# Two products for three where an expert has few tokens, a branch around the third, and experts in pairs

## The chip, the cores and the metric

The kernel runs on one core of one Trainium2 chip. The metric is the device time of one execution in microseconds: a median over runs. The engines of a core that matter here are TensorE (PE, matrix products), VectorE (DVE), ScalarE (ACT) and GpSimd (POOL); each takes its own instructions in the order in which the program put them, and they wait for each other by semaphores. SyncE (SP) issues the transfers of the weights. A profile of one execution shows each instruction's start, duration and what ended the wait ahead of it.

## The reference

A trunk of two pre-norm layers over 256 tokens of width 1024, in float32. Each layer has a token mixer and a channel mixer; the channel mixer of layer 0 is a dense SwiGLU, that of layer 1 chooses two of eight expert SwiGLUs for every token. Each expert has gate and up matrices of 1024 x 3584 and a down matrix of 3584 x 1024:

```
def swiglu(h, w_gate, w_up, w_down):
    return (jax.nn.silu(h @ w_gate) * (h @ w_up)) @ w_down

def moe_ffn(h, router_w, router_b, w_gate, w_up, w_down):
    logits = t.astype(jnp.float32) @ router_w.astype(jnp.float32) + router_b.astype(jnp.float32)
    top_v, top_i = lax.top_k(logits, TOP_K)
    gates = jax.nn.softmax(top_v, axis=-1)
    combine = jnp.sum(jax.nn.one_hot(top_i, N_EXPERTS, dtype=jnp.float32) * gates[..., None], axis=1)
    ...
        y_e = swiglu(t, w_gate[e], w_up[e], w_down[e])
        out = out + combine[:, e:e + 1] * y_e.astype(jnp.float32)
```

The router gives eight counts of tokens that add up to 512. The kernel computes an expert only for its own tokens, in 128 slots; a branch at the end takes care of counts over 128.

## The kernel before

**Products.** A product in float32 precision is made of three products in a rounded type (fp32r): both operands are split into a high and a low part, and `mm3` (lines 152 to 155) adds high x high (L153), low x high (L154) and high x low (L155) in one PSUM bank. In the expert stage the activations are the operand that is loaded (128 x 128), the weights the one that streams (512 columns).

**Weights.** All weights come in blocks of 1 MB into a ring of tiles (`raw`, 11 and 3 more), issued by SP (L104). A block is two pieces. `w_conv` turns a piece into a high part `wh`, a cast on ACT (L119), and a low part `wl` = raw − wh on DVE (L122), each in a ring of four (`NWC`). The first 24 pieces of the experts and the very last ones have a third of the low part done on POOL (L124). `piece` hands out the next piece and converts as far ahead as the rings go.

**Experts.** For each expert, the 3584 hidden columns are seven panels of 512. A panel has three steps of four pieces each: G (gate), D (down, of the panel before) and U (up), in that order (`panel_steps`); the eight experts come one after the other, 56 panels in all. G and U take 24 products each into one bank (`Ge`, `Ue`), D adds 24 into two banks (`edn`) that live through an expert's panels. In the middle of G, `trans` turns the hidden activations of the panel before with four PE transposes (`tre`, L248), and ACT and DVE split the result into `ehh` (L252) and `ehl` (L253). ACT applies silu to `Ge` with the slots' 1/rms as scale (`esg`, L768), and DVE multiplies that by the scaled `Ue` (`eh`, L783).

**Around it.** `one_hot` makes a 0/1 matrix of tokens and slots for a pair of experts, `gather` fetches the pair's tokens by products with it (L686, L687) and splits them into `xte`, `one_hot_T` transposes it; `scatter` takes an expert's results back to the tokens (L712, L713) and adds them, weighted, on DVE (L714). The gathers of the next pair are placed in the second expert's panels. At the end `overflow` loads the largest count (L842) and branches (L843).

The order on each engine is made when the program is built: code in the order in which it is written, except where a scheduler moves instructions of different engines against each other by priority.

## Time and profile before

| | |
|---|---|
| median of 3 runs | 1427.29 us (1425.96 to 1427.61) |
| profiled execution | 1422.7 us of span, 4.6 us around it |
| mean granted clock of PE | 0.993 |
| PE busy | 1391.0 us (98%) |
| DVE busy | 1188.3 us (84%) |
| ACT busy | 968.5 us (68%) |
| POOL busy | 113.6 us (8%) |
| moved by DMA | 428.26 MB, mean 301 GB/s |

Busy times are sums over the whole span. The expert stage is the stretch from 425 to 1409 us; the mixers and the dense layer come before it. Matmuls overlap, so that a busy PE says only that one was under way; the distance between the starts of two of them tells what one costs.

### The profile page before, as it was taken

The numbers are of one execution on the slowest core, as the hardware profiler recorded it, in microseconds if no ns is written. First come the engines' busy times: TensorE is split into PE (matmuls) and PEld (weight loads), VectorE is DVE, ScalarE is ACT, GpSimd is POOL, SyncE is SP. The second block draws the span as 40 slices with busy tenths as digits, with TensorE's granted clock in tenths as the row PEclk, the third lists the DMA queues.
The fourth block names the chain that finished last, engine by engine and source line by source line (L and its number), as shares of the span: only waits on it lengthen the run. The fifth ranks groups of instructions, "written<-read, shape, count | busy, mean of one in ns | idle before, by whom it ended". The sixth has DMA issues, their size and how long they took to land.

```text
span 1422.7 us, 19229 instructions
## 1 busy us (share of the span) xinstructions
PE 1391.0 (98%) x7115; PEld 1173.6 (82%) x7115; DVE 1188.3 (84%) x1304; ACT 968.5 (68%) x1136; POOL 113.6 (8%) x106
## 2 busy tenths in 40 slices
PE   7999999999979999999999999999999999999996
PEld 6989999998957888888888887888887888888884
DVE  6775555558878999999998988999998899999996
ACT  5554444445448887888787777777777777777775
POOL 2311000000338000000000000000000000000002
PEclk9999999999989999999999999999999999999998
DMA  9945555555447999999999999999998999899960
GB/s 364 368 174 178 182 196 184 178 190 186 161 175 265 356 369 373 345 355 351 357 371 356 351 344 350 348 353 370 375 357 335 349 356 350 344 419 359 364 250 32
DMA packets 61301, 428.26 MB, mean 301 GB/s; under 512 B 6928, under 2 KB 7440, under 8 KB 10000
## 3 DMA queue, kind: packets, MB, share of 16 engines
q1 hardware_dynamic: 59904, 424.86, 79.1%
q10 hardware_dynamic: 1008, 1.97, 0.4%
q8 instruction: 57, 0.93, 0.3%
q14 instruction: 44, 0.36, 0.1%
q0 software_dynamic: 288, 0.14, 0.0%
HBM read 425.89 MB, written 1.05 MB: 300 GB/s over the span
## 4 chain that ended last, share of the span: by engine, by line
PE 91%; DVE 4%; issue 2%; ACT 1%; DMA 1%; POOL 0%; ACTq 0%; POOLq 0%; DVEq 0%
PE Ue L155 7%; PE Ue L153 7%; PE Ue L154 7%; PE Ge L153 7%; PE Ge L155 7%; PE Ge L154 7%; PE edn L154 6%; PE edn L155 6%; PE edn L153 6%; DVE wl L122 2%; PE U L295 2%; PE U L294 2%; PE U L293 2%; PE dn L154 2%; PE dn L153 2%; PE dn L155 2%
## 5 line engine op out<-in xcount | busy, mean ns | idle before, releaser
L122 DVE TENSOR_TENSOR wl<-raw,wh 128x1024 fp32r<-128x1024 f32 (+1 forms) x802 | 954.7, 1227 | 147.3 <-ACT wh L119 135.6
L119 ACT CAST wh<-raw 128x1024 fp32r<-128x1024 f32 (+1 forms) x806 | 824.9, 1051 | 290.2 <-PE Ue L154 61.2
L153 PE MATMUL Ge<-wh,xte 128*128 128x512 f32 x448 | 180.5, 403 | 0.0
L155 PE MATMUL Ue<-wl,xte 128*128 128x512 f32 x448 | 175.9, 393 | 3.0 <-DVE wl L122 3.0
L154 PE MATMUL edn<-wh,ehl 128*128 128x512 f32 x448 | 175.0, 391 | 1.6 <-DVE ehl L253 1.6
L155 PE MATMUL Ge<-wl,xte 128*128 128x512 f32 x448 | 175.6, 392 | 0.0
L153 PE MATMUL edn<-wh,ehh 128*128 128x512 f32 x448 | 175.0, 391 | 0.0
L153 PE MATMUL Ue<-wh,xte 128*128 128x512 f32 x448 | 174.6, 390 | 0.0
L154 PE MATMUL Ue<-wh,xte 128*128 128x512 f32 x448 | 174.4, 389 | 0.0
L154 PE MATMUL Ge<-wh,xte 128*128 128x512 f32 x448 | 174.4, 389 | 0.0
L155 PE MATMUL edn<-wl,ehh 128*128 128x512 f32 x448 | 164.3, 393 | 0.2 <-DVE wl L122 0.2
L124 POOL TENSOR_TENSOR wl<-raw,wh 128x320 fp32r<-128x320 f32 x28 | 38.4, 1397 | 962.0 <-PE edn L154 941.2
L155 PEld LDWEIGHTS Ue<-wl,xte 128*128 128x128 f32 x448 | 84.1, 188 | 25.3 <-DVE wl L122 8.1
L155 PEld LDWEIGHTS edn<-wl,ehh 128*128 128x128 f32 x448 | 83.5, 188 | 21.8 <-DVE wl L122 3.6
L154 PEld LDWEIGHTS edn<-wh,ehl 128*128 128x128 f32 x448 | 84.1, 188 | 19.3 <-DVE ehl L253 2.4
L155 PEld LDWEIGHTS Ge<-wl,xte 128*128 128x128 f32 x448 | 84.1, 188 | 18.8
L154 PEld LDWEIGHTS Ue<-wh,xte 128*128 128x128 f32 x448 | 84.1, 188 | 17.5
L153 PEld LDWEIGHTS edn<-wh,ehh 128*128 128x128 f32 x448 | 84.2, 188 | 17.1 <-ACT wh L119 0.2
L153 PEld LDWEIGHTS Ue<-wh,xte 128*128 128x128 f32 x448 | 84.1, 188 | 16.9
L154 PEld LDWEIGHTS Ge<-wh,xte 128*128 128x128 f32 x448 | 84.4, 188 | 16.2
L153 PEld LDWEIGHTS Ge<-wh,xte 128*128 128x128 f32 x448 | 84.2, 188 | 15.6
L252 ACT CAST ehh<-tre 128x512 fp32r<-128x512 f32 x56 | 32.7, 585 | 83.9 <-PE tre L248 83.9
(328 smaller groups left out, 1936.9 us busy)
## 6 DMA issues: line engine op xcount, KB each, us to landing
raw<-in_m_gate_dram SPq DMA_DIRECT2D x112, 1024.0 KB, 7.0
raw<-in_m_up_dram SPq DMA_DIRECT2D x112, 1024.0 KB, 6.5
raw<-in_m_down_dram SPq DMA_DIRECT2D x111, 1024.0 KB, 7.1
raw<-in_w_in_dram SPq DMA_DIRECT2D x15, 1024.0 KB, 5.4
raw<-in_w_gate_dram SPq DMA_DIRECT2D x14, 1024.0 KB, 4.8
raw<-in_w_up_dram SPq DMA_DIRECT2D x14, 1024.0 KB, 4.9
raw<-in_w_down_dram SPq DMA_DIRECT2D x14, 1024.0 KB, 4.8
raw<-in_w_out_dram SPq DMA_DIRECT2D x8, 1024.0 KB, 10.9
```

Of the source, the lines that this page charges most:

```text
L119: nc.scalar.copy(h[:, q], r[:, q])
L122: e.tensor_tensor(lo[:, :cut], r[:, :cut], h[:, :cut].bitcast(F32), op=ALU.subtract)
L124: nc.gpsimd.tensor_tensor(lo[:, cut:], r[:, cut:], h[:, cut:].bitcast(F32), op=ALU.subtract)
L153: nc.tensor.matmul(o, xh, wh, start=start, stop=False)
L154: nc.tensor.matmul(o, xl, wh, start=False, stop=False)
L155: nc.tensor.matmul(o, xh, wl, start=False, stop=stop)
L252: return (nc.scalar.copy(hi, pt), nc.vector.tensor_tensor(lo, pt, hi.bitcast(F32), op=ALU.subtract))
L293: nc.tensor.matmul(o, wh[:, k], hT[:, k], start=k == 0, stop=False)
L294: nc.tensor.matmul(o, wh[:, k], lT[:, k], start=False, stop=False)
L295: nc.tensor.matmul(o, wl[:, k], hT[:, k], start=False, stop=k == KD - 1)
```

## The change

An expert with at most 64 tokens is called light, the others heavy. For a light expert the slots 64 to 127 repeat its tokens (`posm` gets a second form, `one_hot`). Its gathered operand then gets the high parts in slots 0 to 63 and the low parts in slots 64 to 127 (`fold`: ACT scales the second half by `heavy`, DVE adds the low part times `light`). A product of that operand with a piece of weights gives high and low results in different rows of one pass, so that passes with `wh` and `wl` do what three did. The third pass is put in a branch on the expert's count (`third`): eight products that a heavy expert takes and a light one skips. The count of each expert is loaded into PE's registers ahead of the first expert (L829).

The two halves of the rows have to be added. G's and U's results are copied from PSUM by ACT (`eG`, `eU`, L855) and turned with `turn`: eight products in full float32 with a matrix `E` that transposes, adds the halves and applies 1/rms. Silu (L784) and the multiplication (`eh`, L785) come after that. `ehh` and `ehl` are split as before, and a further instruction on DVE (L790) puts the low part into the second half of `ehh` for a light expert.

The steps now run G, U, D (of the panel before), and the two experts of a pair take turns, panel by panel. The rings change: 7 blocks of weights (and 3 more), 8 high parts, 5 low parts, 10 tiles of 512 columns. The results of the two experts are scattered together; the weight of a token is applied to the slots. POOL's share of the first 24 pieces is gone.

```diff
-    NRAW, NWC, NXT = 11, 4, 3
+    NRAW, NWC, NWH = 7, 5, 8
...
-        flat = [(e, n) for e in range(n_exp) for n in range(NPAN)]
+        if n_exp == 1:
+            flat = [(0, n) for n in range(NPAN)]
+        else:
+
+            flat = [(2 * p + j, n) for p in range(n_exp // 2) for n in range(NPAN) for j in range(2)]
         for i, (e, n) in enumerate(flat):
             last = i == len(flat) - 1
             steps.append(("G", e, n))
-            if not last and i > 0:
+            if n_exp == 1 and not last and i > 0:
                 steps.append(("D",) + flat[i - 1])
             steps.append(("U", e, n))
+            if i > 0 and (last or n_exp > 1):
+                steps.append(("D",) + flat[i - 1])
             if last:
-                steps.append(("D",) + flat[i - 1])
                 steps.append(("D", e, n))
         return steps
...
-            h = wp.tile([P, 1024], F32R, tag="wh", name=f"wh{i}", bufs=NWC)
+            h = wp.tile([P, 1024], F32R, tag="wh", name=f"wh{i}", bufs=NWH)
             lo = wp.tile([P, 1024], F32R, tag="wl", name=f"wl{i}", bufs=NWC)
...
-            cut = 704 if i >= 2 * NW - 4 else 704 if moe0 <= i < moe0 + 24 else 1024
+            cut = 704 if i >= 2 * NW - 4 else 1024
...
+        nc.vector.tensor_scalar(light, pr[:, 16:24], 64.5, None, op0=ALU.is_lt)
+        nc.vector.scalar_tensor_tensor(posm[:, :, :, 0], selb, -OFF, pr[:, :16].rearrange("p (b e) -> p b e", b=NB),
                                        op0=ALU.mult, op1=ALU.add)
+        nc.vector.scalar_tensor_tensor(posm[:, :, :, 1], light.unsqueeze(1).to_broadcast([P, NB, NE]), 64.0,
+                                       posm[:, :, :, 0], op0=ALU.mult, op1=ALU.add)
...
         S = sb.tile([P, NB, 2, P], F32R, tag="S", name=f"S{nm}{p}", bufs=1)
-        for b in range(NB):
-            for j in range(2):
-                e = 2 * p + j
-                nc.vector.tensor_scalar(S[:, b, j], iot, posm[:, b, e:e + 1], None, op0=ALU.is_equal)
+        io = iotam.rearrange("p (h t) -> p h t", h=2).unsqueeze(1).to_broadcast([P, 2, 2, 64])
+        for b in range(NB):
+            nc.vector.tensor_tensor(S[:, b].rearrange("p j (h t) -> p j h t", h=2), io,
+                                    posm[:, b, 2 * p:2 * p + 2].unsqueeze(3).to_broadcast([P, 2, 2, 64]),
+                                    op=ALU.is_equal)
...
+        et = sb.tile([P, P], F32, tag="et", name=f"et{nm}", bufs=1)
+        nc.vector.scalar_tensor_tensor(et, swap, light[:, e:e + 1], ident, op0=ALU.mult, op1=ALU.add)
+        E = sb.tile([P, P], F32, tag="E", name=f"E{nm}", bufs=4)
+        nc.vector.tensor_scalar(E, et, rs[:, :1], None, op0=ALU.mult)
+        return ST, rs, E
...
+    def fold(X, e):
+
+        q = (slice(None), slice(None), e % 2, slice(64, P))
+        nc.scalar.activation(X[0][q], X[0][q].bitcast(F32), AF.Copy, scale=heavy[:, e:e + 1])
+        nc.vector.scalar_tensor_tensor(X[0][q], X[1][q].bitcast(F32), light[:, e:e + 1], X[0][q].bitcast(F32),
+                                       op0=ALU.mult, op1=ALU.add)
...
+        def turn(e, n):
+
+            g, u = gs.pop((e, n)), us.pop((e, n))
+            pg, pu = bank("mm", f"gt{e}{n}"), bank("mm", f"ut{e}{n}")
+            for src, o in ((g, pg), (u, pu)):
+                for c in range(4):
+                    q = slice(c * P, (c + 1) * P)
+                    nc.tensor.matmul(o[:, q], src[:, q], E[e], start=True, stop=True)
+            sg, ht = t2(f"esg{e}{n}"), t2(f"eh{e}{n}")
+            nc.scalar.activation(sg, pg, AF.Silu)
+            nc.vector.tensor_tensor(ht, pu, sg, op=ALU.mult)
             hh = t2(f"ehh{e}{n}", F32R).rearrange("p (c t) -> p c t", c=4)
             hl = t2(f"ehl{e}{n}", F32R).rearrange("p (c t) -> p c t", c=4)
-            split(hh, hl, pt.rearrange("p (c t) -> p c t", c=4))
+            h = ht.rearrange("p (c t) -> p c t", c=4)
+            split(hh, hl, h)
+            nc.vector.scalar_tensor_tensor(hh[:, :, 64:], hh[:, :, 64:].bitcast(F32), nlight[:, e:e + 1], h[:, :, 64:],
+                                           op0=ALU.mult, op1=ALU.add)
             hTs[e, n] = (hh, hl)
...
+        def third(e, todo):
+
+            with tc.If(cnt[e] > 64):
+                for o, a, w in todo:
+                    nc.tensor.matmul(o, a, w, start=False, stop=False)
...
         with tc.high_priority():
             begin(0)
             for i in range(4):
                 chunks(0, i)
+            nc.vector.tensor_scalar(heavy, light, -1.0, 1.0, op0=ALU.mult, op1=ALU.add)
+            nc.vector.tensor_copy(cnti, pr[:, 16:24])
+            for e in range(2):
+                fold(X[0], e)
+        nc.vector.tensor_scalar(nlight, light, -1.0, None, op0=ALU.mult)
+        for e in range(NE):
+            cnt[e] = nc.values_load(cnti[0:1, e:e + 1], engines=[mybir.EngineType.PE], min_val=0, max_val=T)
...
             if kind in "GU":
                 pp = bank("mm", f"{kind}e{e}{n}")
+                todo = []
                 for kh in range(4):
                     wh, wl = piece(2)
                     for k in range(2):
-                        kk = kh * 2 + k
-                        mm3(pp, xt[e][:, 0, kk], xt[e][:, 1, kk], wh[:, k], wl[:, k], kk == 0, kk == KD - 1)
-                    if kh == 1 and prev is None:
+                        mm(pp, X[p][0][:, kh * 2 + k, j], wh[:, k], start=kh + k == 0, stop=False)
+                        todo.append((pp, X[p][1][:, kh * 2 + k, j], wh[:, k]))
+                    for k in range(1 if kh == 3 else 2):
+                        mm(pp, X[p][0][:, kh * 2 + k, j], wl[:, k], start=False, stop=False)
+                    if kh == 1:
+                        if kind == "G" and prev is not None:
+                            turn(*prev)
+                        if ready:
+                            (i, ys), more = ready[0], ready[1:]
+                            scatter(ys(), i, f"e{e}")
+                            ready = [(i2, early(y2)) for i2, y2 in more]
+                third(e, todo)
+                mm(pp, X[p][0][:, KD - 1, j], wl[:, 1], start=False, stop=True)
+                t = t2(f"e{kind}{e}{n}")
+                nc.scalar.copy(t, pp)
+                if kind == "G":
+                    gs[e, n] = t
...
+                else:
+                    us[e, n] = t
+                    if e == 0 and n == 0:
+                        route_rest(pr)
                         rest(0)
-                    if kh == 1 and kind == "G" and prev is not None:
-                        trans(*prev)
...
-                if kind == "G":
-                    gt = t2(f"esg{e}{n}")
-                    nc.scalar.activation(gt, pp, AF.Silu, scale=rs[e])
-                    gact[e, n] = gt
...
-                else:
-                    ht = t2(f"eh{e}{n}")
-                    nc.vector.scalar_tensor_tensor(ht, pp, rs[e], gact.pop((e, n)), op0=ALU.mult, op1=ALU.mult)
-                    hs[e, n] = ht
                     prev = (e, n)
...
+            todo = []
             for kk in range(4):
                 wh, wl = piece(1)
                 for i in range(2):
                     q = slice(i * 512, (i + 1) * 512)
-                    mm3(acc[e][i], hh[:, kk], hl[:, kk], wh[:, 0, q], wl[:, 0, q],
-                        n == 0 and kk == 0, n == NPAN - 1 and kk == 3)
-            if n == NPAN - 1:
+                    mm(acc[e][i], hh[:, kk], wh[:, 0, q], start=n == 0 and kk == 0, stop=False)
+                    todo.append((acc[e][i], hl[:, kk], wh[:, 0, q]))
+                if kk < 3:
+                    for i in range(2):
+                        mm(acc[e][i], hh[:, kk], wl[:, 0, i * 512:(i + 1) * 512], start=False, stop=False)
+                if kk == 1 and e == NE - 2 and n == NPAN - 1:
+                    turn(*prev)
+            third(e, todo)
+            for i in range(2):
+                mm(acc[e][i], hh[:, 3], wl[:, 0, i * 512:(i + 1) * 512], start=False, stop=n == NPAN - 1)
```

How instructions stand now is shown at three places. The first is ACT's queue. Before: the casts of G's four pieces (`wh_9021` to `wh_9058`), `ehh`, D's pieces 0 and 1, the silu of G's result, and D's piece 2 (`wh_9099`).

```order
L119 CAST wh_9021<-raw_8719 128x1024
L119 CAST wh_9033<-raw_8719 128x1024
L119 CAST wh_9043<-raw_8744 128x1024
L119 CAST wh_9058<-raw_8744 128x1024
L252 CAST ehh_9083<-tre_9078 128x512
L119 CAST wh_9068<-raw_8775 128x1024
L119 CAST wh_9089<-raw_8775 128x1024
L768 ACTIVATE esg_9109<-Ge_9055,rsle_8483 128x512
L119 CAST wh_9099<-raw_8817 128x1024
```

Now, from the middle of a D step (`wh_7333` is piece 1 of D) through the G step (`wh_7372` to `wh_7398`) to the first piece of U (`wh_7418`):

```order
L137 CAST wh_7333<-raw_7128 128x1024
L855 COPY eU_7368<-Ue_7322 128x512
L137 CAST wh_7343<-raw_7163 128x1024
L137 CAST wh_7351<-raw_7163 128x1024
L814 UNCONDITIONAL_BRANCH
L137 CAST wh_7372<-raw_7181 128x1024
L137 CAST wh_7380<-raw_7181 128x1024
L784 ACTIVATE esg_7444<-gt_7434 128x512
L137 CAST wh_7390<-raw_7210 128x1024
L137 CAST wh_7398<-raw_7210 128x1024
L137 CAST wh_7418<-raw_7228 128x1024
```

The silu has moved from D into G, where it reads the turned gate (`gt`) and stands ahead of the cast of piece 2; in D its place is taken by the copy of U's result (`eU`).

The second is PE's queue in the middle of a G step. Before (`wh_9033` is piece 1, `wh_9043` piece 2):

```order
L153 MATMUL Ge_9055<-wh_9033,xte_7652 128x512
L154 MATMUL Ge_9055<-wh_9033,xte_7652 128x512
L155 MATMUL Ge_9055<-wl_9034,xte_7652 128x512
L248 MATMUL tre_9078<-con,eh_9053 128x128 x4
L153 MATMUL Ge_9055<-wh_9043,xte_7652 128x512
L154 MATMUL Ge_9055<-wh_9043,xte_7652 128x512
L155 MATMUL Ge_9055<-wl_9044,xte_7652 128x512
```

Now (`wh_7372` is piece 0, `wh_7380` piece 1):

```order
L841 MATMUL Ge_7415<-wh_7372,xe_4781 128x512 x2
L782 MATMUL gt_7434<-Ee_6454,eG_7320 128x128 x4
L844 MATMUL Ge_7415<-wl_7373,xe_4781 128x512 x2
L841 MATMUL Ge_7415<-wh_7380,xe_4781 128x512 x2
L782 MATMUL ut_7435<-Ee_6454,eU_7368 128x128
L844 MATMUL Ge_7415<-wl_7381,xe_4781 128x512 x2
L782 MATMUL ut_7435<-Ee_6454,eU_7368 128x128 x3
L841 MATMUL Ge_7415<-wh_7390,xe_4781 128x512 x2
```

Two passes stand where three stood; the turn's eight products with `Ee` lie between pieces 0 and 2.

The third is the end of a U step on PE. Before (`wh_9011` is the last piece):

```order
L155 MATMUL Ue_9008<-wl_9012,xte_7652 128x512
L153 MATMUL Ue_9008<-wh_9011,xte_7652 128x512
L154 MATMUL Ue_9008<-wh_9011,xte_7652 128x512
L155 MATMUL Ue_9008<-wl_9012,xte_7652 128x512
L153 MATMUL Ge_9055<-wh_9021,xte_7652 128x512
```

Now, with the branch (`wh_7303` and `wl_7304` are the last piece) and the first products of D:

```order
L841 MATMUL Ue_7322<-wh_7303,xe_4781 128x512 x2
L844 MATMUL Ue_7322<-wl_7304,xe_4781 128x512
L814 COMPARE_AND_BRANCH
L816 MATMUL Ue_7322<-wh_7258,xe_4782 128x512 x2
L816 MATMUL Ue_7322<-wh_7266,xe_4782 128x512 x2
L816 MATMUL Ue_7322<-wh_7295,xe_4782 128x512 x2
L816 MATMUL Ue_7322<-wh_7303,xe_4782 128x512 x2
L814 UNCONDITIONAL_BRANCH x2
L853 MATMUL Ue_7322<-wl_7304,xe_4781 128x512
L904 MATMUL edn_7043<-wh_7325,ehh_7288 128x512
L904 MATMUL edn_7044<-wh_7325,ehh_7288 128x512
L908 MATMUL edn_7043<-wl_7326,ehh_7288 128x512
```

The low x high products of all four pieces have moved behind the others and into the branch, and one product with `wl` follows it.

## Rows read from the trace of the kernel before

**Rows 1.** The page: span; busy time by engine; DMA rate in 40 slices.

```profile
span 1422.7 us, 19229 instructions
...
PE 1391.0 (98%) x7115; PEld 1173.6 (82%) x7115; DVE 1188.3 (84%) x1304; ACT 968.5 (68%) x1136; POOL 113.6 (8%) x106
...
GB/s 364 368 174 178 182 196 184 178 190 186 161 175 265 356 369 373 345 355 351 357 371 356 351 344 350 348 353 370 375 357 335 349 356 350 344 419 359 364 250 32
```

**Rows 2.** Windows: busy time (instructions) by engine, granted clock, DMA share, GB/s.

```profile
core 0: us, PE busy (x) PEld busy (x) DVE busy (x) ACT busy (x) POOL busy (x), PEclk, DMA share, GB/s
600.00:700.00 100.00, 100.00 (x466) 82.98 (x465) 94.64 (x105) 80.81 (x95) 0.00 (x0) 1.00 0.93 353
...
400.00:430.00 30.00, 21.92 (x119) 15.70 (x117) 22.70 (x63) 13.20 (x31) 12.39 (x10) 0.83 0.25 91
```

**Rows 3.** The waits: who for whom, us in total, times, longest.

```profile
DVE wl L122 <- ACT wh L119: 135.6, 192, 1.9
ACT wh L119 <- PE Ue L154: 61.2, 194, 0.6
PEld Ue L155 <- DVE wl L122: 8.1, 14, 0.8
```

**Rows 4.** Timeline of PE, one panel: start, duration, instruction.

```profile
start us, us, engine line op out<-in xcount [idle before <-releaser]
...
702.43 0.39 PE L153 MATMUL Ge<-wh,xte 128*128 128x512 f32 x1
...
704.93 0.39 PE L155 MATMUL Ge<-wl,xte 128*128 128x512 f32 x1
...
705.16 0.60 PE L248 MATMUL tre<-con,eh 128*128 128x128 f32 x4
...
707.91 0.39 PE L154 MATMUL Ge<-wh,xte 128*128 128x512 f32 x1
...
719.24 0.39 PE L153 MATMUL Ge<-wh,xte 128*128 128x512 f32 x1
```

**Rows 5.** Timeline of DVE in the same panel.

```profile
703.28 0.74 DVE L783 SCALAR_TENSOR_TENSOR eh<-Ue,rsle,esg 128x512 f32<-128x512 f32 x1
703.94 3.50 DVE L122 TENSOR_TENSOR wl<-raw,wh 128x1024 fp32r<-128x1024 f32 x3
707.35 0.68 DVE L253 TENSOR_TENSOR ehl<-tre,ehh 128x512 fp32r<-128x512 f32 x1
...
709.42 1.23 DVE L122 TENSOR_TENSOR wl<-raw,wh 128x1024 fp32r<-128x1024 f32 x1 [0.17 <-ACT wh L119]
```

**Rows 6.** Timeline of ACT in the same panel.

```profile
705.13 1.05 ACT L119 CAST wh<-raw 128x1024 fp32r<-128x1024 f32 x1 [0.30 <-PE Ge L154]
706.08 0.58 ACT L252 CAST ehh<-tre 128x512 fp32r<-128x512 f32 x1
...
708.33 1.06 ACT L119 CAST wh<-raw 128x1024 fp32r<-128x1024 f32 x1 [0.33 <-PE Ge L154]
709.30 0.67 ACT L768 ACTIVATE esg<-Ge,rsle 128x512 f32<-128x512 f32 x1
```

**Rows 7.** A product in full fp32 (timeline of PE), and its reader (tile mix).

```profile
36.35 0.83 PE L358 MATMUL mix<-vn,wsT 128*128 128x128 f32 x6
...
L362 DVE SCALAR_TENSOR_TENSOR yb<-mix,par,u x16: 340/343/353, 37.4 to 355.4; 128x128 f32<-128x128 f32 x16
```

**Rows 8.** Lines 842 and 843: a count loaded and compared, on the engines' queues.

```profile
L842 SPq TENSOR_LOAD <-cmax x1: 467/467/467, 420.6 to 420.6; - x1
L842 SPq FUSED_REGOPS  x1: 186/186/186, 421.1 to 421.1; - x1
L842 PEldq TENSOR_LOAD <-cmax x1: 484/484/484, 1411.0 to 1411.0; - x1
...
L843 PEldq COMPARE_BRANCH  x1: 3422/3422/3422, 1411.6 to 1411.6; - x1
L843 PEldq EVENT_SEMAPHORE  x1: 51/51/51, 1415.1 to 1415.1; - x1
L843 POOLq COMPARE_BRANCH  x1: 45/45/45, 1415.4 to 1415.4; - x1
...
L843 SPq COMPARE_BRANCH  x1: 50/50/50, 1416.6 to 1416.6; - x1
```

**Rows 9.** Timeline of PE: the first expert product, and the first after the last.

```profile
425.27 0.58 PE L153 MATMUL Ge<-wh,xte 128*128 128x512 f32 x1
...
1408.96 0.40 PE L712 MATMUL poe<-yhe,STe 128*128 128x512 f32 x1
```

More of the change, by code (lines that the diff above doesn't have):

```diff
@@ L90, in trunk_kernel, with raw_tag @@
     HALF = (0, 2 * NW - 1)
-    raws, conv, pos = {}, {}, [0, 0, 0]
+    raws, conv, pos, slots = {}, {}, [0, 0, 0], {}
+    def raw_tag(i):
+        if extra:
+            j = i - extra[1]
+            if j < 2:
+                return "xo", 2
+            if (j - 2) % (NRAW + 1) == 0 and i < NW - 30:
+                return "rx", 1
+        return "raw", NRAW
     def w_dma(j, between=None):
@@ L126, in w_conv @@
             pos[1] += 1
+            if i % 2:
+                del raws[i // 2], r
     def piece(k, hold=False):
@@ new lines, in rest, with both, early @@
+        def rest(p):
+            for e in (2 * p, 2 * p + 1):
+                ST[e], rs[e], E[e] = one_hot_T(Sp[p], e, f"e{e}")
+        def both(e, i):
+            return lambda: [(ST[m], y_split(acc[m][i], rs[m], i, f"e{m}")) for m in (e, e + 1)]
+        def early(ys):
+            r = ys()
+            return lambda: r
+        def third(e, todo):
+            with tc.If(cnt[e] > 64):
+                for o, a, w in todo:
+                    nc.tensor.matmul(o, a, w, start=False, stop=False)
@@ L742, in moe @@
+        mm = nc.tensor.matmul
         with tc.high_priority():
```

190 lines of the change are left out of this document (100 added, 90 removed).

## Prediction

> **What bounds the kernel now.** I read the page first, then the windows of the expert stage, the waits, and last one expert panel instruction by instruction. TensorE (PE) is busy 1391.0 of 1422.7 us, VectorE (DVE) 84%, ScalarE (ACT) 68% [rows 1]. In the expert stage PE is busy 100% at clock 1.00, DVE 95%, ACT 81%, and 353 GB/s of weights come in [rows 2], where one stretch of the page shows 419 GB/s [rows 1]. DVE's largest wait is for ACT's casts, 135.6 us, and ACT itself waits for PE to hand back buffers; PE hardly waits for DVE, 8.1 us at its largest such place [rows 3]. So PE's own products set the time, and DVE has little to spare. A panel (G, U and D of 512 columns) starts every 719.24 − 702.43 = 16.81 us; products follow each other every (704.93 − 702.43)/11 = 0.227 us, and a panel's 72 of them with four transposes (0.60 − 0.27 over three steps, 0.11 each) make 16.8 [rows 4]. Nothing is left over: PE never stops in a panel. A pair of panels takes 33.62.
>
> **The units.** A product's result stands 0.39 after its start [rows 4]. A low part (DVE) takes 1.22 and follows the one before by 1.135 (three in 3.50); any DVE or ACT instruction starts about 0.09 before the end of the one ahead, as ehl does (703.94 + 3.50 against 707.35) [rows 5]. A high part (ACT) takes 1.05 and follows by 0.95, a copy or cast of 512 columns 0.58 (by 0.49), a silu 0.67 (by 0.58) [rows 6]. A reaction across engines is 0.03 to 0.04: PE's product at 707.91 ends at 708.30 and the cast starts at 708.33; that ends at 709.39, and DVE starts at 709.42 [rows 4 to 6].
>
> **What is removed and added, as sums.** With the reference's inputs the experts get 60, 67, 66, 51, 74, 63, 71 and 60 tokens, so each pair has one light (at most 64) and one heavy expert. A light panel loses 24 of its 72 products. Each panel swaps four transposes (0.43) for eight products in full fp32 of 128 columns, two passes each at (0.83 − 0.275)/5 = 0.111 [rows 7]: 1.79. PE's products per pair of panels: 48 + 72 at 0.227 and 2 × 1.79, 30.8. Ahead of each of the three branches of a light panel PE waits until its last product is through: 0.39 − 0.23 of a product, an event of 0.05, a near compare-and-branch of 0.05 (POOL's 45 ns) [rows 8], and a weight load that nothing covers, which I put at the spacing 0.23: 0.5 each, bounds 0.2 (only the product's end) and 1.2. That gives 32.4. DVE: 24 × 1.135 and, per panel, eh, ehl (0.61 each) and the fold (256 elements a partition, between 0.34 for 128 [rows 7] and 0.74 for 512 [rows 5], so 0.48, by 0.40): 30.5. ACT: 24 × 0.95 + 2 × (3 × 0.49 + 0.58) = 26.9. DMA: 12.58 MB at 419 GB/s [rows 1], 30.0. By these sums the new bound is PE's 32.4, 1.2 us below today.
>
> **What the order makes of them.** The sums hold only if casts run ahead of PE across a panel. In the new order ACT's eU copy stands in front of the casts of D's pieces 2 and 3, and the silu in front of those of G's pieces 2 and 3; both wait for results that PE has only just produced, and DVE can't split a piece that ACT hasn't cast. Before, the silu stood in the same place of D: behind G's end the cast of piece 2 was done by 0.43 + 0.58 + 1.05 = 2.06 and its low part by 3.3, but PE came for it only after sixteen products, at 3.9. Two passes bring PE there six products earlier. So I follow each step by hand; time 0 is the start of the last product of the step before.
> D: U's result is there at 0.39, eU starts at 0.43, the cast of piece 2 at 0.92, done 1.97; its low part runs 2.01 to 3.23. PE wants it after ten products, at 0.227 + 10 × 0.227 = 2.49, and gets it at 3.27: it stalls 0.78. Piece 3's is in time.
> G: two products, then four of the gate's turn; the last of these starts at 0.23 + 0.45 + 0.67 = 1.35 and is through at 1.74. Silu starts at 1.78, the cast of piece 2 at 2.36, done 3.41; low part 3.45 to 4.67. PE is there after 10 products and all 8 of the turn, at 4.28: it stalls 0.43, and 0.23 more at piece 3, since two low parts (2 × 1.135) take longer than two pieces of two passes (4 × 0.227 each).
> U of a light expert (DVE now carries the rest): DVE ends piece 3's low part, then eh, until 6.33 on G's scale, and only then starts U's piece 0; PE (G took 6.59) stalls 0.33 and 0.23 at pieces 0 and 1, then 1.24 at piece 2, which stands behind ehl and fold (0.61 + 0.40), and 0.23 at piece 3. U of a heavy one starts 1.35 later: 0.44 and 0.23.
> Lengths, as products + turn + stalls + drain (0.5 light, 0.05 heavy): G light 3.63 + 1.79 + 0.66 + 0.5 = 6.6, U light 3.63 + 2.03 + 0.5 = 6.2, D heavy 5.44 + 0.78 + 0.05 = 6.3, G heavy 5.44 + 1.79 + 0.66 + 0.05 = 7.9, U heavy 5.44 + 0.67 + 0.05 = 6.2, D light 3.63 + 0.78 + 0.5 = 4.9. A pair of panels takes 38.0 in place of 33.62: 28 × 4.4 = +123 us. The same bookkeeping on the order of before gives no stall and 16.75 a panel, against 16.81 in the trace, which is why I trust it. With a drain of 0.2 it is 37.4, with 1.2 it is 39.4; with a reaction twice as long 38.5: 28 times these, −17, +39 and +14 us.
>
> **The rest.** From the first G product to the first product after the last D are 1408.96 − 425.27 = 983.7 us [rows 9], 42 more than 56 × 16.81: gathers, scatters, the last pieces. Their PE products stay but for small ones; the inserts on ACT and DVE now delay a conversion one for one. I take 50, bounds 40 and 60: +8 (−2 to +18). At the start eight loads of a count stand on PE between the last gather and the first G, where before the two were interleaved: 0.47 to 0.48 each with 0.19 of register work behind it [rows 8], 5.3, or the chain of cast, low part and two folds if that is longer: +6 (3 to 9). Ahead of the experts the rings change but not the work; PE's whole idle time in the span is 31.7 us [rows 1], and I take 0. Fewer raw buffers (10 in place of 14) cost nothing as long as 12.58 MB take 38 us: 331 GB/s, less than the 353 of now.
> Sum: the profiled execution, 1422.7 of span and 4.6 around it, is 1427.3, the median of the runs too. 1427.3 + 123 + 8 + 6 = 1564 us. Own range 1500 (half of the stalls vanish) to 1620 (long drains).
>
> **Rivals.**
> (a) Faster: the five low parts and eight high parts that may be ahead do run ahead, and PE's content decides: 28 × (32.4 − 33.6) = −34, + 14 from the rest: about 1407; with free branches 28 × (30.8 − 33.6) + 14, 1363. For it: the sums, in which DVE and ACT lie below PE. Against it: ACT takes its queue in order, and the copy ahead of the casts can't start before PE has ended U. It decides where low parts of pieces 2 and 3 are done before eU's result is; the order rules it out in the steady panels.
> (b) Much slower, by the branch. In the trace the only taken branch on PE, at the end, held it 3.42 us, against 0.045 on POOL and 0.05 on SP for theirs [rows 8]. If each of the 84 light branches cost that: 84 × (3.42 − 0.05) = +283, about 1847. Against it: PE's branch at the end skips a long body, these skip eight products. [...]
> (c) Slower by the clock: From 400 to 430 PE was busy 21.9 of 30 us, and the granted clock was 0.83 on average [rows 2]. If the gaps here, up to 1.24 in a panel, brought that mean: 30.8 × 0.2 = 6 us on each pair of panels, +173, about 1737. Against it: the gaps here are far shorter, and PE stays busy 85%.
> (d) No change: stalls worth 0.6 a pair of panels rather than 5.6.
> (e) The third pass isn't skipped (all counts above 64): the counts say otherwise; the same steps with two heavy experts give 40.7 a pair, about 1640.
>
> **Chances.** Forecast's mechanism, 1500 to 1620: 0.62. Stalls partly hidden, 1431 to 1500: 0.09. (b), (c), (e) together: 0.08. (d), within 0.2% or ±2.9 us, about what a measurement of this kernel can tell from no change: 0.04. (a): 0.17. So faster 0.17, same 0.04, slower 0.79. The range over all of it runs from 1405, with half of (a) inside, to 1620, and leaves out some 0.17.
>
> **What would show it.** In the changed profile: panels every 19 us; PE busy about 85% of the expert stage, idle before U's, G's and D's low-part products with DVE's wl as releaser, 0.8 in each D, most in U of the light experts; ACT waiting for PE at the eU copy and at the silu; DVE waiting for ACT's casts; weights at about 330 GB/s; near branches of 0.05 to 0.1 with a gap of some 0.5 around each light one; clock 1.00. It is wrong if PE shows no idle time ahead of piece 2 in D, if panels come at 16.2 (a), or if PE's gaps sit at the branch rather than at low parts (b).

## The result and the profile after

The changed kernel takes 1535.01 us (median of 4 runs, 1534.16 to 1536.13); the kernel before, 1426.62 (1425.75 to 1427.61). The ratio is 1.0763, with a 95% interval of 1.0747 to 1.078. The forecast was 1564 in a range of 1405 to 1620: right in sign and in kind, 29 us too slow.

The page after: the span, busy time by engine, and the DMA rate in 40 slices (as [rows 1]).

```profile
span 1534.3 us, 19463 instructions
...
PE 1413.8 (92%) x7122; PEld 1109.4 (72%) x7123; DVE 1188.8 (77%) x1335; ACT 989.9 (65%) x1222; POOL 80.8 (5%) x82
...
GB/s 366 249 145 192 192 178 182 191 186 156 179 165 308 344 347 321 325 305 303 338 326 327 327 327 321 319 323 331 328 323 326 331 328 318 330 330 324 323 309 30
```

TensorE has 23 us more of busy time, though 24 products fewer in each light panel; DVE has the same sum. In the windows of the expert stage (columns as in [rows 2]) every engine now has idle time, and the weights come slower:

```profile
1300.00:1400.00 100.00, 91.56 (x394) 64.60 (x395) 81.78 (x80) 72.37 (x86) 0.00 (x0) 1.00 0.88 328
```

Nothing is at its limit: PE 92%, DVE 82%, ACT 72%, DMA 88%, at clock 1.00. (The prediction's 85% was a sum of spacings from start to start. A busy share also counts the end of the last product ahead of each gap, 0.39 against 0.23; with about fourteen gaps in a pair of panels that is 14 × 0.16 = 2.2 of 38 us, or 6 points.) The waits say who waits for whom (us in total, times, longest; PEld is PE's queue of weight loads):

```profile
DVE wl L140 <- ACT wh L137: 148.8, 86, 3.8
ACT esg L784 <- PE gt L782: 127.1, 50, 4.5
ACT eU L855 <- PE Ue L853: 121.9, 54, 4.1
PEld Ue L844 <- DVE wl L140: 83.1, 126, 1.7
PEld edn L908 <- DVE wl L140: 57.4, 86, 1.3
...
PE Ue L844 <- DVE wl L140: 33.6, 47, 1.3
...
PE edn L908 <- DVE wl L140: 23.6, 45, 0.9
```

DVE's wait for casts was there before, at 135.6 [rows 3]. New are the rows below it: ACT waits for the turn's products (silu, L784) and for U's last product (the copy, L855), 2.5 and 2.3 us on average at nearly each of the 56 panels, and PE's products and weight loads wait for low parts in U and D, where the largest such wait was 8.1 in all [rows 3]. The timeline of PE shows where, first in a D step (a row with x2 or x8 merges that many products, and its start is that of the first):

```profile
1347.60 0.61 PE L904 MATMUL edn<-wh,ehh 128*128 128x512 f32 x2
1348.06 0.67 PE L908 MATMUL edn<-wl,ehh 128*128 128x512 f32 x2
1348.57 0.63 PE L904 MATMUL edn<-wh,ehh 128*128 128x512 f32 x2
1349.72 0.73 PE L908 MATMUL edn<-wl,ehh 128*128 128x512 f32 x2 [0.53 <-DVE wl L140]
1350.29 0.62 PE L904 MATMUL edn<-wh,ehh 128*128 128x512 f32 x2
1350.75 1.99 PE L816 MATMUL edn<-wh,ehl 128*128 128x512 f32 x8
```

Steps of 0.46 and 0.51 up to 1348.57, then 1.15 to the product at 1349.72, which waits for the low part of piece 2: 0.69 lost, where the prediction had 0.78. The two products that start there take 0.57 instead of 0.46. In U of the light expert the same piece, again on PE:

```profile
1381.15 0.63 PE L841 MATMUL Ue<-wh,xe 128*128 128x512 f32 x2
1382.84 0.73 PE L844 MATMUL Ue<-wl,xe 128*128 128x512 f32 x2 [1.06 <-DVE wl L140]
```

From 1381.15 to 1382.84 it is 1.69 in place of 0.47, so 1.22 lost; predicted were 1.24. The timelines of ACT and of DVE for one such pair of steps (start, duration, instruction, what ended the idle time before) show the cause:

```profile
901.86 0.59 ACT L855 COPY eU<-Ue 128x512 f32<-128x512 f32 x1 [3.42 <-PE Ue L853]
902.34 3.89 ACT L137 CAST wh<-raw 128x1024 fp32r<-128x1024 f32 x4
908.14 0.60 ACT L784 ACTIVATE esg<-gt 128x512 f32<-128x512 f32 x1 [1.91 <-PE gt L782]
908.63 3.88 ACT L137 CAST wh<-raw 128x1024 fp32r<-128x1024 f32 x4
```

```profile
903.42 4.63 DVE L140 TENSOR_TENSOR wl<-raw,wh 128x1024 fp32r<-128x1024 f32 x4 [1.99 <-ACT wh L137]
909.70 2.36 DVE L140 TENSOR_TENSOR wl<-raw,wh 128x1024 fp32r<-128x1024 f32 x2 [1.64 <-ACT wh L137]
```

ACT stands idle for 3.42 us in front of the copy, with four casts behind it that need only a buffer; as soon as PE ends U, the copy and the four casts run back to back. DVE's low parts start 1.08 after the first of those casts, having waited 1.99. The silu does the same 6.3 us later. Weights to convert are there, engines to convert them are idle, and one instruction at the head of ACT's queue holds them.

The heavy expert's G starts at 1353.03 and again at 1391.30:

```profile
1353.03 0.63 PE L841 MATMUL Ge<-wh,xe 128*128 128x512 f32 x2
...
1391.30 0.63 PE L841 MATMUL Ge<-wh,xe 128*128 128x512 f32 x2
```

They are 38.27 apart, and so are those of each plain pair of panels (the fourth pair of experts, beside which no gather runs). Before it was 33.62.

### The profile page after: what moved, and what is told of

Read it like the earlier page. It is cut to its first block, busy times and chain, and to the rows that moved or that the text cites. A ratio compares the mean times of both kernels' runs of the same rounds, so it can differ in the third digit from the quotient of the medians.

```text
span 1534.3 us, 19463 instructions
## 1 busy us (share of the span) xinstructions
PE 1413.8 (92%) x7122; PEld 1109.4 (72%) x7123; DVE 1188.8 (77%) x1335; ACT 989.9 (65%) x1222; POOL 80.8 (5%) x82
## 5 line engine op out<-in xcount | busy, mean ns | idle before, releaser
L140 DVE TENSOR_TENSOR wl<-raw,wh 128x1024 fp32r<-128x1024 f32 x802 | 945.4, 1223 | 229.9 <-ACT wh L137 148.8
L844 PE MATMUL Ue<-wl,xe 128*128 128x512 f32 x392 | 140.4, 428 | 34.6 <-DVE wl L140 33.6
L841 PE MATMUL Ge<-wh,xe 128*128 128x512 f32 x448 | 147.6, 408 | 6.8 <-DVE xe L743 4.6
L844 PE MATMUL Ge<-wl,xe 128*128 128x512 f32 x392 | 143.8, 437 | 3.1
L841 PE MATMUL Ue<-wh,xe 128*128 128x512 f32 x448 | 141.7, 398 | 0.1
L844 PEld LDWEIGHTS Ue<-wl,xe 128*128 128x128 f32 x392 | 67.5, 189 | 91.2 <-DVE wl L140 83.1
L784 ACT ACTIVATE esg<-gt 128x512 f32<-128x512 f32 x56 | 33.5, 598 | 127.1 <-PE gt L782 127.1
L855 ACT COPY eU<-Ue 128x512 f32<-128x512 f32 x56 | 32.9, 587 | 121.9 <-PE Ue L853 121.9
L841 PEld LDWEIGHTS Ge<-wh,xe 128*128 128x128 f32 x448 | 81.2, 191 | 23.0 <-DVE xe L743 4.8
L841 PEld LDWEIGHTS Ue<-wh,xe 128*128 128x128 f32 x448 | 82.7, 189 | 19.4 <-ACT wh L137 2.9
L782 PEld LDWEIGHTS ut<-Ee,eU 128*128 128x128 f32 x448 | 66.0, 190 | 9.6 <-issue 0.5
L782 PE MATMUL ut<-Ee,eU 128*128 128x128 f32 x448 | 67.2, 274 | 0.2 <-PEq L814 0.2
```

The costliest lines, as they stand in the source:

```text
L140: e.tensor_tensor(lo[:, :cut], r[:, :cut], h[:, :cut].bitcast(F32), op=ALU.subtract)
L782: nc.tensor.matmul(o[:, q], src[:, q], E[e], start=True, stop=True)
L784: nc.scalar.activation(sg, pg, AF.Silu)
L841: mm(pp, X[p][0][:, kh * 2 + k, j], wh[:, k], start=kh + k == 0, stop=False)
L844: mm(pp, X[p][0][:, kh * 2 + k, j], wl[:, k], start=False, stop=False)
L855: nc.scalar.copy(t, pp)
```

## The experiments

Theory 1: the order of ACT's and DVE's in-order queues makes the loss; conversions wait behind an instruction that waits for PE. Theory 2: the branches do (a drain, in which PE waits until its last product is through: at one light D that product ends at 465.09 and the branch's semaphore event stands at 465.1; a fence that the scheduler doesn't move instructions across). Theory 3: the smaller rings or the later DMA do. Theory 4: the pairing itself. "Plain" below is the pair of panels without inserts, the instructions of gathers, scatters and the next pair's tables. In the conditions on order, `issue_after(x)` puts an instruction behind x in its engine's queue; nothing else changes.

### Undo the order on ACT: e1_casts_first, and its halves

```diff
-                nc.scalar.copy(h[:, q], r[:, q])
+                casts[i] = nc.scalar.copy(h[:, q], r[:, q])
...
-            nc.scalar.activation(sg, pg, AF.Silu)
+            with tc.issue_after(casts[min(pos[2] + 1, pos[1] - 1)].ins):
+                nc.scalar.activation(sg, pg, AF.Silu)
...
-                nc.scalar.copy(t, pp)
+                if kind == "U":
+                    with tc.issue_after(casts[min(pos[2] + 3, pos[1] - 1)].ins):
+                        nc.scalar.copy(t, pp)
+                else:
+                    nc.scalar.copy(t, pp)
```

The copy then stands behind the cast of D's last piece and the silu behind that of G's. e1a_copy_only has only the edit of the copy, e1b_silu_only only that of the silu.

> The changed kernel with two orders on ACT: the copy of U's result (eU) stands behind the casts of all four D pieces instead of behind two, and the silu behind the casts of all four G pieces instead of behind two. Nothing else is moved, and no work is added or left out. Theory 1 (ACT's in-order queue: a result of PE stands ahead of casts that PE needs next): the stalls of D (0.78) and of G (0.43 + 0.23) go; by the same bookkeeping, with the drain of 0.30 that the trace shows, a pair of panels goes from 37.6 to 33.4, so 4.2 less on the 26 pairs that show the pattern: -109, about 1426 us, panels paired at about 34.0. Theory 2 (the branches, with their drain and what they split, set the time): no more than 15 us less, 1520 to 1535. Theory 3 (weights arrive too late from a ring of 7 and 3 blocks): no change, 1535.

> Only the copy of U's result goes behind the casts of all four D pieces; the silu stays. Theory 1: D's stall goes in both experts, part of it comes back in G, where the silu still stands ahead of piece 2's cast: 37.6 to 36.45 a pair of panels, -30, about 1505. Theories 2 and 3: 1530 to 1535.

> Only the silu goes behind the casts of all four G pieces; the copy of U's result stays. Theory 1: G's stalls go and most of U's with them, since DVE has U's first low parts earlier; D keeps 0.78: 37.6 to 34.7 a pair of panels, -77, about 1458. Theories 2 and 3: 1530 to 1535.

Measured: e1_casts_first 1459.69 (ratio to before 1.0239, 1.0222 to 1.0256), e1a_copy_only 1501.49 and e1b_silu_only 1493.0 (one run each). So two moved instructions give back 75 of the 109 us; the halves give 34 and 42, which add up to it. The copy's half came as expected, the silu's was a miss: 42 where 77 were expected, with a plain pair of 35.58 in place of 34.7. With both, the plain pair is 34.10, as expected of it; that the whole stayed 34 us above 1426 lies in the pairs with inserts (35 to 39) and the start. The waits of e1_casts_first:

```profile
DVE eh L786 <- PE ut L782: 66.6, 46, 1.6
PEld Ue L845 <- DVE wl L140: 44.2, 58, 1.6
...
ACT eU L858 <- PE Ue L854: 36.7, 31, 2.2
ACT xe L733 <- PE pxe L730: 31.5, 15, 4.5
```

The copy's wait fell from 121.9 to 36.7, the low parts' in U from 83.1 to 44.2. A new one stands on DVE: `eh` (L786), which waits for the turn's last product and holds low parts, 66.6 us at 46 places.

### The next in the queue: e2_eh_later

```diff
-            nc.vector.tensor_tensor(ht, pu, sg, op=ALU.mult)
+            with tc.issue_after(lows[min(pos[2] + 2, pos[1] - 1)].ins):
+                nc.vector.tensor_tensor(ht, pu, sg, op=ALU.mult)
```

with the edits of e1_casts_first, and `lows[i]` kept at the low parts as `casts[i]` at the casts: `eh` stands behind the first low parts of U.

> e1_casts_first with one more move: eh on DVE stands behind the low parts of U's pieces 0 and 1 (before: behind those of G), because in e1 DVE now waits 1.6 us in front of eh in every panel with low parts left to do. Theory 1 (a wait in front of conversions on an in-order queue is the cost, now on DVE): the stall of U's piece 2 (0.8 in e1) and some of the gather panels' loss go; plain pairs from 34.1 to 33.5, gather pairs more: -20 to -35 us against e1, 1425 to 1440. Rival (DVE is simply full: 30.5 us of work in 34): no more than -5, about 1455 to 1460.

Measured 1462.4 (1.0253, 1.0236 to 1.027): a miss as a whole. The window says that the edit did its work where nothing else runs:

```profile
1300.00:1400.00 100.00, 98.65 (x460) 77.29 (x459) 92.61 (x92) 82.08 (x98) 0.00 (x0) 1.00 0.99 376
```

PE is nearly full again, the plain pair is 33.17, 0.93 less than in e1_casts_first. But the pairs beside a gather went from 35.1 to 35.4 up to 36.1 to 36.4 in the second and third pair of experts, and the waits name the next instruction of the same kind: the gather's split on ACT, which waits for PE's gather (31.5 in e1_casts_first, 15.3 in the changed kernel):

```profile
ACT xe L733 <- PE pxe L730: 44.7, 14, 4.5
```

### The same for the gather, with larger rings: e8_rings, e9_gather_later, e10_rest_later

e8_rings is e2_eh_later with one buffer moved from raw weights to each of the two rings of converted ones:

```diff
-    NRAW, NWC, NWH = 7, 5, 8
+    NRAW, NWC, NWH = 6, 6, 9
```

e9_gather_later adds to it that the gather's copies and folds stand behind the conversions of the next U (`behind` enters `issue_after`, as above):

```diff
-            nc.scalar.activation(X[0][:, i * 2 + c], px[:, c], AF.Copy, scale=g)
+            with behind(casts, 3, tag == 'mm' and nm[0] == 'e'):
+                nc.scalar.activation(X[0][:, i * 2 + c], px[:, c], AF.Copy, scale=g)
...
-        nc.scalar.activation(X[0][q], X[0][q].bitcast(F32), AF.Copy, scale=heavy[:, e:e + 1])
+        with behind(casts, 3, e > 1):
+            nc.scalar.activation(X[0][q], X[0][q].bitcast(F32), AF.Copy, scale=heavy[:, e:e + 1])
```

and likewise the two on DVE. e10_rest_later does it for the small tables of the next pair too (`ST`, `rs`, `E`):

```diff
-        nc.scalar.copy(ST, pst[:, :T].rearrange("p (b t) -> p b t", b=NB))
+        with behind(casts, 3, e > 1 and nm[0] == 'e'):
+            nc.scalar.copy(ST, pst[:, :T].rearrange("p (b t) -> p b t", b=NB))
```

> e2_eh_later with other rings: 6 low parts for 5, 9 high parts for 8, 6 blocks of weights for 7 (all that the memory holds). Theory 1 with the same bookkeeping: rings don't bind once casts run ahead, no change in plain pairs, a little in gather pairs: 0 to -10 us against e2. Rival (the depth of the low-part ring is what stops DVE): -20 or more. Theory 3 (weights late): slower, since there are fewer blocks ahead.

> e8_rings with the inserts for the next pair (the gathered operand's high and low part, and its fold) put behind the high and low parts of all four U pieces on ACT and DVE; before, ACT waited there for the gather's products (up to 4.5 us once) with casts behind it. Theory 1: pairs of panels with a gather go from 36.1 to 36.4 towards the plain 33.2, by 1 to 2.5 each in 12 of them: -12 to -30 us against e8_rings, 1425 to 1443. Rival (the gather's own work, on PE and DVE, is what they cost): no more than -5.

> e9_gather_later with the last of the next pair's inserts (the slots' matrix, 1/rms and E) put behind U's conversions as well; in e9 ACT waits 2.7 and 1.6 us there and DVE 3.0 and 2.8, and those three pairs of panels take 37.7 to 39.2 in place of 34. Theory 1: 2 to 4 us less in each of the three: -6 to -12 against e9, 1421 to 1428, level with the kernel before or a little below it. Rival (the work of these inserts costs, not where they stand): no more than -2, about 1432.

Measured: e8_rings 1454.59 (one run), 8 less than e2_eh_later with the plain pair unchanged at 33.2. The pairs beside a gather didn't change either (36.41 and 36.1 in both); the second and fourth pair of panels are 2.2 and 3.1 shorter, and each change of experts 0.7. With fewer blocks of raw weights it was faster, which speaks against theory 3 in this stage. e9_gather_later 1433.8 (1.0058, 1.0042 to 1.0075): the pairs with a gather fell from over 36 to 33.9 to 34.2, as expected. Left are the pairs in which one pair of experts ends and the next begins, 37.6 to 39.5 each. e10_rest_later 1432.63 (1.0044, 1.0031 to 1.0058), a miss: the pairs at the end of two pairs of experts got shorter (39.21 to 37.08, 37.65 to 35.07), those at the start of two longer (39.5 to 40.73, 37.71 to 40.62). Part of this is only where the boundary falls: 4 and 12 products of D (0.9 and 2.8 us) now come behind the next pair's first G. Over a whole change of experts it is +1.4, +0.8 and −2.2. In the first two PE now waits once for 3.48 us:

```profile
913.04 1.19 PE L861 MATMUL Ue<-wh,xe 128*128 128x512 f32 x2 [3.48 <-DVE eh L805]
```

The granted clock is 0.99 from 450 to 700, where e9_gather_later has 1.00, and 0.985 over the span, there 0.991. So one change of experts lost its wait, and in the other two a wait stands at a new place. From the changed kernel to here, 102 of 109 us came back, some 94 by the order of the queues alone and 8 by the rings. The window of e9_gather_later and its largest wait on this path:

```profile
1300.00:1400.00 100.00, 98.65 (x464) 77.77 (x463) 92.52 (x92) 81.99 (x97) 0.00 (x0) 1.00 0.95 360
```

```profile
ACT esg L798 <- PE gt L795: 75.5, 49, 4.1
```

The silu still waits for the turn (75.5), but with the casts ahead of it, and PE is as full as in the window of e2_eh_later.

### The branch: e3_no_branch

```diff
-            with tc.If(cnt[e] > 64):
+            if e in (1, 2, 4, 6):
```

The third pass is fixed when the kernel is built, by the inputs' counts; the loads of the counts stay.

> The changed kernel without the 168 branches of the third pass: whether an expert takes it is fixed when the program is built, by the counts of the reference's inputs (the eight loads of the counts stay). Theory 1: the drain goes, 0.30 in each of 84 light steps, -25 at most, and the ACT queue keeps its copy ahead of two casts of D (the silu is behind four casts in some panels now, which gives some of the 2.9 a pair back): 1470 to 1515, D's stalls still there. Theory 2: the branches are what costs: back to the content of PE, 30.8 a pair, about 1430 or less. Theory 3: 1510 to 1535.

Measured 1472.45 (1.0326, 1.0309 to 1.0343): 62.6 less, within what was expected, plain pair 36.49, 31.8 in the first experts. But this run doesn't measure the branch alone: without branches as fences the scheduler also set the silu behind all four casts in some panels, which is e1b's edit in part (from 1330.36 six casts run on ACT between the copy and the silu, where the change has four). The branch by itself is read from the change's profile. At one light D, on PE, and then the branches' own row on the queue (ns: shortest, median, longest):

```profile
464.48 0.61 PE L904 MATMUL edn<-wh,ehh 128*128 128x512 f32 x2
465.24 0.70 PE L913 MATMUL edn<-wl,ehh 128*128 128x512 f32 x2
```

```profile
L814 PEldq COMPARE_BRANCH  x253: 65/169/335, 437.2 to 1518.1; - x127
```

The products before and behind the branch lie 0.53 apart (the second of the two at 464.48 starts 0.23 later, at 464.71, the next at 465.24) where 0.23 is the spacing: 0.30 for a branch that is taken. In light G and U the same two products lie 0.64 apart (1377.72 and 1378.36), in heavy ones, where the branch falls through, the products there lie 0.33 (1358.57 and 1358.90); there the low part of the last piece comes late in both, and the difference is 0.31 again. In a heavy D, where it falls through, no gap shows.

### Both, for these counts: e11_no_branch_best

The edit of e3_no_branch on e10_rest_later.

> e10_rest_later without the 168 branches (whether an expert takes the third pass is fixed when the program is built, by the counts of the reference's inputs). Now that the conversions keep up, PE's own time shows: the trace of the changed kernel has 0.53 between the starts of the products around a light branch, where products follow each other by 0.23. Theory 1: 84 x 0.30 = -25 against e10, 1396 to 1404, plain pairs of panels at 32.3 for 33.2. Rival (conversions still bind, and take back what PE saves): no more than -10.

Measured 1413.33 (0.9914, 0.9899 to 0.9929): 12 us or 0.9% less than the kernel before, and 19.3 less than e10_rest_later, where all drains together are 84 × 0.30 = 25. That lies between the theory (−25) and its rival (−10). The plain pair is 32.77, 0.40 shorter where its three drains are worth 0.9; of the 19.3, 6.1 come from the third pair of panels (38.24 to 32.17), which had stayed at 38.2 in the changed kernel and in all its orders above. With the order repaired, the branches cost 19 us; but this kernel holds only for inputs with these light and heavy experts. None that decides it on the chip beat the kernel before.

### The pairing: e6_unpaired

```diff
-            flat = [(2 * p + j, n) for p in range(n_exp // 2) for n in range(NPAN) for j in range(2)]
+            flat = [(e, n) for e in range(n_exp) for n in range(NPAN)]
```

The one turn that D takes over near the end is moved to the panel that needs it then; nothing else is edited.

> The changed kernel with the experts one after the other again (light and heavy panels no longer take turns); all else as changed. Theory 1: the stalls belong to each panel's own order, and by the same bookkeeping two light panels (34.5) and two heavy (40.7) make the same 37.6 a pair: 1525 to 1545 us, and DVE and ACT wait in the same places. Rival (the turns of light and heavy panels are a cost, or hide one): more than 20 us away on either side.

Measured 1537.67 (one run), 2.7 from the change. The waits are the same ones, to a few us:

```profile
DVE wl L140 <- ACT wh L137: 147.1, 86, 3.1
ACT esg L784 <- PE gt L782: 127.5, 49, 3.4
ACT eU L855 <- PE Ue L853: 123.6, 50, 4.2
```

Within this one run, the pairing costs nothing and gives nothing.

### The fold on GpSimd: e5_pool_fold

On e2_eh_later, the fold of `eh` in two GpSimd instructions, to relieve DVE:

```diff
-            nc.vector.scalar_tensor_tensor(hh[:, :, 64:], hh[:, :, 64:].bitcast(F32), nlight[:, e:e + 1], h[:, :, 64:],
-                                           op0=ALU.mult, op1=ALU.add)
+            nc.gpsimd.tensor_scalar(hh[:, :, 64:], hh[:, :, 64:].bitcast(F32), nlight[:, e:e + 1], None, op0=ALU.mult)
+            nc.gpsimd.tensor_tensor(hh[:, :, 64:], hh[:, :, 64:].bitcast(F32), h[:, :, 64:], op=ALU.add)
```

> e2_eh_later with the fold of ehh (one DVE instruction of 0.48 us a panel) as two GpSimd instructions, which had nothing to do there. Theory 1: what DVE no longer carries ends U's low parts 0.4 earlier: -0.4 to -0.8 a pair, 10 to 20 us below e2. Rival (the fold, now about 2 us long by the 1.4 us of a subtraction of 320 columns there, becomes late for D): D starts late behind ehh, 0 to +40 us against e2.

Measured 1509.29 (1.0583, 1.0565 to 1.0601), 47 more than e2_eh_later: the rival was right, and by more than it said. The largest new wait of PE's queues:

```profile
PEld edn L910 <- POOL ehh L793: 56.3, 31, 5.6
```

D's first weight load waits for the fold, 56.3 us at 31 places. Two GpSimd instructions of 1.75 and 1.15 us (medians) took the place of one of 0.48 on DVE, and the fold stands on the path from `eh` to D. In plain pairs it costs only 0.5 (33.65 for 33.17); the rest lies outside the plain pairs. And a part is the clock: its mean over the span is 0.973 in place of 0.989. The missing 0.016 of 1506.5 is 24 us, so that by this estimate up to half of the 47 can be products at a lower granted clock; the two aren't separated.

### The start: e7_before_raw7

The kernel before with its first ring of raw weights cut from 11 buffers to 7, as the change has it:

```diff
-    NRAW, NWC, NXT = 11, 4, 3
+    NRAW, NWC, NXT = 7, 4, 3
```

> The kernel before with 7 blocks of weights in the first ring instead of 11; nothing else. In the changed kernel the products of the router come 4.8 us later than before, and PE is idle 2.9 us more between 40 and 120 us, where the weights come in at 229 in place of 329 GB/s. Theory A (the shorter ring reads less ahead before the dense layer, whose start then waits for weights): the same 3 to 5 us here, in the same stretch, and the expert panels unchanged at 16.81: 1429 to 1432. Theory B (the deeper rings of high and low parts shift the order there): no change, 1425 to 1428.

Measured 1424.78 (0.9997, 0.9987 to 1.0007): no change. The ring of raw weights isn't what made the part ahead of the experts 5.6 us longer; theory 3 has no support there. The other rings weren't tried, and this loss stays open.

## Why the prediction came out as it did

**What bounds it.** Right. The bound moved from PE's products to the order of conversions on ACT and DVE.

**Steps of a panel.** Right, nearly each: G, U and D of the light expert measured 6.49, 6.27 and 4.92 (predicted 6.6, 6.2, 4.9), of the heavy one 7.97, 6.26 and 6.36 (7.9, 6.2, 6.3). A pair takes 38.27 against 38.0. Following each queue instruction by instruction found the stalls of piece 2 to a tenth; the sums by engine, which gave 32.4, would have said faster. The term of +123 is 28 × (38.27 − 33.62) = +130.2.

**The branch.** Mis-sized: 0.30 a light step where I took 0.5, inside the bounds of 0.2 and 1.2. The stalls in G and in heavy U were shorter too, 0.47 and 0.46 against 0.66 and 0.67. The lengths still came out, because products came slower: 0.233 apart in G and U, and some 0.1 later behind each late low part. That the pair fits to 0.3 is in this part luck: errors of both signs. The compare-and-branch itself was longer than forecast (median 0.169 where 0.05 to 0.1 was said). What a branch keeps the scheduler from doing wasn't in the prediction.

**The rest: the step that failed.** The prediction put gathers, scatters and last pieces at 50 in place of 42, "the inserts on ACT and DVE now delay a conversion one for one": +8, bounds −2 and +18. The stage from the first G product to the first after the last D is 1520.60 − 437.17 = 1083.4 us; less 28 × 38.27 that leaves 11.8, so −30.5. Two reasons, read from the starts of G in the trace. Inserts ran in time in which the engines waited anyway: pairs beside a gather take 38.5 to 39.3, 0.25 to 1.0 more than plain ones, where in the kernel before each single panel beside a gather took 17.8 to 18.7, 1.0 to 1.9 more than the plain 16.81. And the first three pairs took 97.1 together, 12.8 less than three plain ones would (one D is not in them, 4.9): I take it that ACT had casts in stock there until its waits ran it dry, which no run tested. The rest of the 30.5 isn't divided further.

**The start.** From the products that count the slots (`prank`) to the first G product it is 437.17 − 424.59 = 12.58 us, before 6.24: +6.3 as predicted (+6), by loads and chain together. The rows of PE, then the loads on its queue and the last fold on DVE:

```profile
424.59 0.17 PE L646 MATMUL prank<-selb,tri_b 128*128 128x8 bf16 x1 [6.36 <-DVE selb L627]
...
437.17 1.22 PE L841 MATMUL Ge<-wh,xe 128*128 128x512 f32 x2 [4.60 <-DVE xe L743]
...
441.59 0.96 PE L844 MATMUL Ge<-wl,xe 128*128 128x512 f32 x2
442.39 0.63 PE L841 MATMUL Ge<-wh,xe 128*128 128x512 f32 x2
```

```profile
L829 PEldq TENSOR_LOAD <-cnti x8: 299/303/488, 431.4 to 436.5; - x8
L829 PEldq FUSED_REGOPS  x8: 146/146/160, 432.0 to 436.9; - x8
L829 PEldq SEQ_ASSERT  x8: 18/18/32, 432.2 to 437.1; - x8
```

```profile
435.20 1.41 DVE L743 SCALAR_TENSOR_TENSOR xe<-xe,light,xe 128x512 fp32r<-128x512 f32 x2 [0.56 <-ACT xe L742]
```

Eight loads of 0.30 and 0.15 of register work, 0.73 from one to the next, end at 437.1; the fold on DVE ends at 436.61, and a reaction across engines took 0.03 to 0.04 in the trace of before [rows 4 to 6]. The row names DVE, but the loads, on PE's own queue, end last; without them the chain of gather, split and fold would have let the first product start some 0.5 earlier. Both terms that the prediction named are there, nearly equal. The clock comes on top, in the stage itself: behind 4.60 us without work products come 0.427 apart until 442.39, and the granted clock of that stretch is 0.50; it is 1.00 behind it. The windows (columns as in [rows 2]; the first two are at the start, the third behind another gap of 3.87 us near the end):

```profile
437.20:442.30 5.10, 5.10 (x12) 4.08 (x13) 2.45 (x2) 0.00 (x0) 0.00 (x0) 0.50 0.20 26
442.50:464.00 21.50, 21.20 (x107) 17.44 (x106) 18.45 (x24) 18.17 (x23) 0.00 (x0) 1.00 0.67 246
1511.30:1518.00 6.70, 6.60 (x15) 4.56 (x15) 4.60 (x7) 0.00 (x0) 0.00 (x0) 0.54 0.00 0
```

Twelve products at 0.427 in place of 0.23 are 2.4 us. Ahead of `prank` nothing was to change, but its products came at 424.59 instead of 419.03: +5.6 where the prediction had 0.

Together: 130.2 − 30.5 + 6.3 + 5.6 = 111.6, the difference of the spans, 1534.3 − 1422.7.

**Rivals.** (a), faster by the sums: fell, for the reason given; e11_no_branch_best, 1413.33, shows what of it was there once order and branches were out. (b), 3.42 us a branch: fell. The near branches' longest is 0.335 and their median 0.169. Why the one at the end held PE for 3.42 [rows 8], no run shows. (c), the clock: fell, with 1.00 in the window of plain panels; it was lower at the start (0.50) and the end (0.54), and briefly in the stage (0.98 from 940 to 1040 and from 1040 to 1140). (d) and (e) fell with the pair's length and with the light panels' missing pass.

**Why the change can't win much here.** The plain pair with its order repaired and branches kept takes 33.17, against 33.62: the 24 products saved (24 × 0.227 = 5.4) go to two turns in place of two groups of transposes (2 × (1.70 − 0.43) = 2.5), three drains (0.9), and products of G and U that come 0.233 apart (80 × 0.006 = 0.5); by difference, 1.1 is left for stalls at low parts. A turn whole, on PE in e11_no_branch_best:

```profile
1223.07 1.05 PE L800 MATMUL gt<-Ee,eG 128*128 128x128 f32 x8
1223.96 1.06 PE L800 MATMUL ut<-Ee,eU 128*128 128x128 f32 x8
1224.77 0.72 PE L861 MATMUL Ge<-wh,xe 128*128 128x512 f32 x2
```

28 × 0.45 is some 12 us. In e9_gather_later 5.2 of them are left: from its first G product to the first after its last D it is 978.5, before 983.7. The rest goes where no plain pairs run, above all where experts change; where in those pairs isn't settled. But its first G product comes at 438.28, before at 425.27: 13.0 later. So what e9_gather_later still loses, 7.8 of span, lies ahead of the first expert product, not in the expert stage.

## What to carry to other kernels

When work is taken from the engine that bounds a kernel, walk the queues of the others again: an instruction that waits for the bound engine must stand behind all that the bound engine needs next, and the slack that hid a wrong order goes with the work removed. Compare sums by engine only after that; here they gave 1407 us for a kernel of 1535. A wait that is removed at the head of an in-order queue shows the next one of its kind (here the copy's wait fell from 121.9 to 36.7 us, and 66.6 at `eh` were new), so such an edit is judged in a plain stretch first, and then over the inserts.

## What the runs showed of the hardware

- Eight loads of a count on PE took 0.73 us each from start to start: 0.30 (one 0.488), 0.146 of register work, the rest between. The kernel before had single loads of 0.467 and 0.484, with 0.186 behind one of them [rows 8].
- A taken branch past eight products on PE set the products around it 0.30 us further apart (0.53 for 0.23, at 464.71 and 465.24); the compare-and-branch itself took 65 to 335 ns.
- Behind 4.60 us without a product on PE the granted clock of the next 5.1 us was 0.50; behind 3.87 us it was 0.54 over the next 6.7.
- GpSimd's fold of 256 columns took 2.9 us in two instructions (medians of 1.75 and 1.15), against 0.48 in one on DVE.
- Products that wait for their low part come some 0.1 later than others, as the two of 0.73 us at 1349.72 against 0.62 for the two behind them. PE's load for the first of them starts together with it, at 1349.72; the next load starts at 1350.06, 0.23 ahead of its product at 1350.29.
- Eight products of 512 columns follow each other every 0.227 us in some G steps and every 0.233 in others. In e11_no_branch_best the first and third pair of experts have the one, the second and fourth the other:

```profile
614.76 1.98 PE L836 MATMUL Ge<-wh,xe 128*128 128x512 f32 x8
...
1226.50 2.03 PE L836 MATMUL Ge<-wh,xe 128*128 128x512 f32 x8
```

The gathered operand of these pairs lies in tiles of different names (`big` and `xo`, in `x_tiles`). Whether the place makes the difference wasn't tested.
